# Two interleaved input products, wider zero matmuls, a shifted job queue and one more pre-scaled norm chunk in a two-layer decoder trunk

## The chip, the cores and the metric

The kernel runs on one core of one Trainium2 chip. The metric is the device time of one launch in microseconds (us), as a median over runs. PE is the matrix engine (PEld its weight loads), DVE the vector engine, ACT the scalar engine, POOL the GpSimd engine, and SP the queue from which most transfers are issued.

## The reference, cut to what matters

The input `x` has 256 positions and 2048 channels, all in float32. Two layers follow each other, each ending in a residual and a LayerNorm.

```python
# layer 0: one wide input projection feeds two head groups
z, xbc, dt, q, k, v, gate = split(x @ w_in)
xbc = silu(causal_depthwise_conv(xbc, conv_w, conv_b))   # 4 taps
xs, B, C = split(xbc)                                    # B, C: 4 groups x 128 states
y_a = rms_norm((ssd_scan(xs, dt, B, C) + d * xs) * silu(z))
y_b = moba_attention(rotary(q), rotary(k), v) * silu(gate)
x = layer_norm(alpha * x + concat(y_a, y_b) @ w_out)
# layer 1: diagonal complex state space mixer
u, gate = split(x @ w_in1)
y = gelu(s5(u, lam_re, lam_im, log_dt, b, c) + d * u)
ga, gb = split(y @ w_glu)
x = layer_norm(alpha * x + ((ga * sigmoid(gb)) * silu(gate)) @ w_out1)
```

B and C are the columns called `b` and `c` below, 512 columns each.

## The kernel before, in words

Every large product is float32 made of three single-pass matmuls: both operands are split into a high part (a copy rounded to the matrix engine's fast format) and a low part (the rest), and high·high, high·low and low·high are added up. Weights come in *units* of 128 x 1024 numbers (512 KB): two contraction tiles of 128 rows by 512 output columns. `split_to(i)` (lines 205 to 229) issues the transfer of each unit up to the i-th into a `raw` tile, makes `wh` on ACT (line 225) and `wl` on DVE (line 227). There are four buffers of each. It is called three units ahead of the one that PE works on. For unit 0 the same is done in two halves (lines 216 to 218), each together with one tile of `x` (`xpart`, lines 411 to 413).

`product("w", ...)` runs over the eight units of one block of 512 columns and calls `wmm` (line 288): 24 matmuls per unit, each of 128 x 128 weights against 256 positions, into two PSUM banks. Two pairs of banks alternate from product to product. `product("x", ...)` (line 271) has the operands the other way round: 12 matmuls of 512 columns per unit.

The first product makes `b`, the second `c`, four more make `xs`, four make `z`, then 16 make q, k, v and gate. While the first product runs, `x` arrives in pieces of two tiles (`xpiece`, lines 397 to 403): the dictionary `early` puts piece i ahead of unit i, and piece 5 also issues the constants and parameters.

All other work hangs in a queue of jobs. After each unit `pump` takes as many jobs off the queue as are needed to empty it by the end of the product, and `run` (line 243) places a job behind the split of the unit two ahead. A scheduler then orders each engine's instructions. The jobs that matter here are: four convolution taps and a SiLU per 512 columns (`conv_jobs`, ACT line 506, DVE line 509), the `dt` product and softplus (`dt_mm` lines 424 to 431, `dt_jobs` lines 443 to 493), the C·B masks (`cb_job`, lines 530 to 534), and the tables of the second layer (`trig_job` lines 551 to 575, `table_job` lines 581 on). Later, `block_jobs` build the second layer's matrices block by block; each of 16 blocks loads 256 KB of parameters into one buffer (`bc<-in_s5bc`, line 650).

PE starts with `warm(WARM0)` (line 367): 70 matmuls of zeros, 64 x 64, into an unused bank.

Between the layers lies a border. The last output product of layer 0 (`product_apart`) finishes rows 0 to 127 (t = 0) first and rows 128 to 255 (t = 1) afterwards. `after0` adds the residual (line 973), takes statistics (line 974, 990 to 993) and scales 512-column chunks of the normed row in two DVE steps (`scaled`, lines 1013 and 1016). `turned` transposes a chunk on PE (line 358) and splits it on ACT (line 1026) and DVE (line 1030). For t = 1 PE has to wait for this chain, and `warm(WARM1)` and `warm(WARM2)` put 30 and 4 further matmuls of zeros there. The first product of layer 1 starts when the first chunks are turned; `rest0` turns the remaining half chunk between the terms of its unit 0, and `later` turns further chunks ahead of units 1, 3 and 5, as `step(t, chunk)`, which is `scaled` and then `turned`.

Of the kernel before, what the change touches and what calls it, by code (L numbers as in the profile page):

```python
# [9 lines left out]
F32 = mybir.dt.float32  # L10
F32R = mybir.dt.float32r
AF = mybir.ActivationFunctionType
OP = mybir.AluOpType
# [3 lines left out]
P = 128  # L17
# [3 lines left out]
UK = 2  # L21
CU = KT // UK
ALPHA = 4.0 ** 0.25
NKEEP = 6
WARM0 = 70
WARM1 = 30
WARM2 = 4
EPS = 1e-5
# [65 lines left out]
def _layout(inp):  # L94
# [15 lines left out]
    a["wi0"] = np.concatenate([_chunk(m) for m in cols], 0)  # L110
    w = f["out0_w"][0].reshape(32, P, D)
# [48 lines left out]
def trunk(tc, io, out):  # L160
# [8 lines left out]
    with ExitStack() as top:  # L169
# [30 lines left out]
        nsplit = [0]  # L200
        early = {}
        splits = {}
        keep = [None, range(0)]

        def split_to(i):
            while nsplit[0] <= min(i, len(units) - 1):
                n = nsplit[0]
                if n in early:
                    early.pop(n)()
                raw = st.tile([P, UK, 512], F32, tag="raw", name=nm("raw"))  # L210
                if n == 0:
                    wh = st.tile([P, UK, 512], F32R, tag="wh", name=nm("wh"))
                    wl = st.tile([P, UK, 512], F32R, tag="wl", name=nm("wl"))
                    for k in range(UK):
                        xpart(k)
                        nc.sync.dma_start(raw[:, k, :], units[n][:, k * 512 : k * 512 + 512])
                        A.activation(wh[:, k, :], raw[:, k, :], AF.Copy)
                        V.tensor_tensor(wl[:, k, :], raw[:, k, :], wh[:, k, :].bitcast(F32), op=OP.subtract)
                    ready[n] = (wh, wl)
                    nsplit[0] += 1  # L220
                    continue
                nc.sync.dma_start(raw.rearrange("p k n -> p (k n)"), units[n])
                pool, th, tl = (keep[0], f"wh{n % 8}", f"wl{n % 8}") if n in keep[1] else (st, "wh", "wl")
                wh = pool.tile([P, UK, 512], F32R, tag=th, name=nm("wh"))
                high = A.activation(wh, raw, AF.Copy)  # L225
                wl = pool.tile([P, UK, 512], F32R, tag=tl, name=nm("wl"))
                splits[n] = (high, V.tensor_tensor(wl, raw, wh.bitcast(F32), op=OP.subtract))  # L227
                ready[n] = (wh, wl)
                nsplit[0] += 1
# [42 lines left out]

        def wmm(ps, u, nu, hl, wpair, late=None):
            pv = [p.rearrange("p (f n) -> p f n", n=S) for p in ps]
            wh, wl = wpair
            steps = [(j, o) for j in range(UK) for o in range(4)]
            if u == nu - 1:
                steps = [(j, o) for o in range(4) for j in range(UK)]
            for terms in ((0, 2), (1,)) if late else ((0, 1, 2),):
                if late and terms == (1,):  # L280
                    late()
                for j, o in steps:
# [8 lines left out]

        def product(kind, hl, nu=CU, prelude=None, late=None):
            ps = banks()
            for u in range(nu):
# [4 lines left out]
                if kind == "w":  # L299
                    wmm(ps, u, nu, hl, wpair, late if u == 0 else None)  # L300
                else:
# [59 lines left out]
        idle = cst.tile([P, 64], F32R, name="idle")  # L361
        G.memset(idle.bitcast(F32), 0.0)

        def warm(n):
            px = aux()
            for i in range(n):
                T.matmul(px[:64, 0:64], idle, idle, start=i == 0, stop=i == n - 1)  # L367

# [12 lines left out]
        with ExitStack() as l0:  # L381
# [24 lines left out]
            for i in range(1, CU):  # L406
                early[i] = xpiece(i)

# [108 lines left out]
            cT = a4([P, 4, S])  # L517
            ps = product("w", xhl)
            conv_jobs(ps, 0, bT)
            jobs.append(dt_mm)  # L520
            jobs.extend(dt_jobs())
            ps = product("w", xhl)
            conv_jobs(ps, 4, cT)
            fmem = big("F", [P, 4096])
            cbm = fmem[:, 0:1536].rearrange("p (g n) -> p g n", g=4)

            def cb_job(g):
# [7 lines left out]
                return go  # L535

            for g in range(4):
                jobs.append(cb_job(g))

# [185 lines left out]

            jobs.extend([trig_job, table_job])
            xs = big("C", [P, 2, D])
# [3 lines left out]
            def xs_jobs(ps, j):  # L731
# [263 lines left out]
        with ExitStack() as lt:  # L995
# [41 lines left out]
            def after0(ps, t):  # L1037
# [289 lines left out]
```

## Time and profile before

| what | value |
| --- | --- |
| time, median of 3 runs | 1364.88 us (1363.3 to 1366.78) |
| the profiled execution's own time | 1366.41 us |
| its span, first to last instruction | 1364.6 us |
| PE busy | 1349.1 us in 9918 matmuls |
| DVE, ACT, POOL busy | 982.8, 673.3, 372.3 us |
| transfers | 283.02 MB, mean 207 GB/s |
| mean granted PE clock | 0.995 |

A row of the timeline has the start, the length, the engine, the source line, the operation, output and input, the count, and in brackets how long the engine had been idle and what ended that. The length of a matmul in such rows is modelled and overlaps the next one; what PE really needs per matmul is the distance between two starts. A row of the windows view gives a stretch and its length, then for each engine the busy time and the number of instructions, and at the end the granted PE clock, the share of the transfer engines and GB/s. A row of the chain gives start, length and the instructions that followed each other without a gap.

### The profile page before, as it was taken

To read this page: it belongs to the slowest core of one execution; us is meant where nothing else is said; L and a number is where in the kernel's file an instruction comes from. 1 tells how busy PE (TensorE), PEld (TensorE's weight loads), DVE (VectorE), ACT (ScalarE), POOL (GpSimd) and SP (SyncE) were. 2 spreads that over 40 slices of the span, in tenths; PEclk is the share of its full clock that TensorE was granted. 3 is DMA by queue.
4 is the path that set the end of the run, shared out by engine and by line. 5 is a ranking of instruction groups with operands and counts; after the bars stand their busy time and mean duration, and the time that the engine had idled before them with its cause. 6 is when DMAs were issued, how large, how long until landed. Compare 5 with 4: busy or idle time off the path is not lost.

```text
span 1364.6 us, 25068 instructions
## 1 busy us (share of the span) xinstructions
PE 1349.1 (99%) x9918; PEld 1214.1 (89%) x9918; DVE 982.8 (72%) x1559; ACT 673.3 (49%) x869; POOL 372.3 (27%) x649
## 2 busy tenths in 40 slices
PE   9999999999999999999999999999999999999996
PEld 9999999998998998998988888899977788888885
DVE  5789746687688779689788766748788856555555
ACT  5565557764543543554554344344344545444441
POOL 0140000123027628616788700013243100000001
PEclk9999999999999999999999999899999999999998
DMA  8556555545546756756767779397888666666762
GB/s 308 173 156 201 176 169 166 155 140 170 184 125 208 254 164 205 261 169 207 256 203 229 216 231 315 121 303 247 288 269 300 210 211 191 187 189 187 256 215 78
DMA packets 80742, 283.02 MB, mean 207 GB/s; under 512 B 9840, under 2 KB 12528, under 8 KB 80112
## 3 DMA queue, kind: packets, MB, share of 16 engines
q1 hardware_dynamic: 68112, 239.33, 55.5%
q0 software_dynamic: 7328, 30.42, 6.8%
q10 hardware_dynamic: 5184, 11.67, 2.2%
q8 instruction: 78, 1.28, 0.4%
q14 instruction: 40, 0.33, 0.1%
HBM read 260.41 MB, written 20.97 MB: 206 GB/s over the span
## 4 chain that ended last, share of the span: by engine, by line
PE 94%; DVE 4%; DMA 1%; issue 1%; ACT 0%; POOL 0%; POOLq 0%; DVEq 0%
PE main L288 43%; PE main L271 43%; DVE wl L227 1%; PE aux L358 1%; PE enc L1131 1%; PE aux L794 1%; PE dec L1176 1%; PE aux L701 1%; PE aux L367 1%; DMA bc<-in_s5bc 1%; PE aux L906 1%; PE aux L874 1%; PE aux L764 0%; PE dec L1172 0%; PE aux L697 0%
## 5 line engine op out<-in xcount | busy, mean ns | idle before, releaser
L227 DVE TENSOR_TENSOR wl<-raw,wh 128x1024 fp32r<-128x1024 f32 x431 | 538.5, 1251 | 329.5 <-ACT wh L225 323.4
L225 ACT ACTIVATE wh<-raw 128x1024 fp32r<-128x1024 f32 x431 | 456.1, 1059 | 579.1 <-PE main L271 266.0
L288 PE MATMUL main<-A,wh 128*128 128x256 f32 x1408 | 402.6, 286 | 0.0
L288 PE MATMUL main<-B,wh 128*128 128x256 f32 x1408 | 400.1, 284 | 0.0
L288 PE MATMUL main<-A,wl 128*128 128x256 f32 x1408 | 399.9, 284 | 0.0
L288 PEld LDWEIGHTS main<-A,wh 128*128 128x128 f32 x1408 | 270.8, 192 | 0.6 <-issue 0.2
L288 PEld LDWEIGHTS main<-B,wh 128*128 128x128 f32 x1408 | 270.8, 192 | 0.4
L288 PEld LDWEIGHTS main<-A,wl 128*128 128x128 f32 x1408 | 270.7, 192 | 0.2 <-issue 0.2
L271 PE MATMUL main<-wl,A 128*128 128x512 f32 x512 | 200.4, 391 | 0.5 <-DVE wl L227 0.3
L271 PE MATMUL main<-wh,A 128*128 128x512 f32 x512 | 200.4, 392 | 0.0
L271 PE MATMUL main<-wh,B 128*128 128x512 f32 x512 | 200.0, 391 | 0.0
L271 PE MATMUL main<-wh,C 128*128 128x512 f32 x384 | 152.0, 397 | 0.0
L271 PE MATMUL main<-wh,F 128*128 128x512 f32 x384 | 150.0, 391 | 0.0
L271 PE MATMUL main<-wl,C 128*128 128x512 f32 x384 | 149.8, 390 | 0.0
L635 POOL TENSOR_TENSOR c<-c 128x8 f32<-128x8 f32 (+2 forms) x192 | 108.0, 581 | 28.8 <-DMA wb<-c 21.3
L271 PEld LDWEIGHTS main<-wl,A 128*128 128x128 f32 x512 | 96.2, 188 | 20.9 <-DVE wl L227 1.3
L271 PEld LDWEIGHTS main<-wh,B 128*128 128x128 f32 x512 | 96.2, 188 | 19.9
L271 PEld LDWEIGHTS main<-wh,A 128*128 128x128 f32 x512 | 96.2, 188 | 19.8 <-issue 0.2
L271 PEld LDWEIGHTS main<-wh,C 128*128 128x128 f32 x384 | 72.1, 188 | 15.5
L271 PEld LDWEIGHTS main<-wh,F 128*128 128x128 f32 x384 | 72.1, 188 | 15.4
L271 PEld LDWEIGHTS main<-wl,C 128*128 128x128 f32 x384 | 72.1, 188 | 14.3
L804 POOL TENSOR_TENSOR ssq<-ssq,c 128x256 f32<-128x256 f32 x16 | 17.6, 1099 | 210.2 <-ACT c L802 209.6
(279 smaller groups left out, 1680.6 us busy)
## 6 DMA issues: line engine op xcount, KB each, us to landing
raw<-in_wi SPq DMA_DIRECT2D x271, 512.0 KB, 4.0
raw<-in_wo SPq DMA_DIRECT2D x96, 512.0 KB, 4.3
raw<-in_wglu SPq DMA_DIRECT2D x64, 512.0 KB, 3.7
wt<-wb POOLq DMA_DIRECT2D x16, 896.0 KB, 7.6
wb<-ob ACTq DMA_DIRECT2D x16, 512.0 KB, 5.5
bc<-in_s5bc SPq DMA_DIRECT2D x16, 256.0 KB, 4.4
wb<-c POOLq DMA_DIRECT2D x16, 256.0 KB, 4.1
wb<-om ACTq DMA_DIRECT2D x16, 128.0 KB, 4.1
```

The lines of the kernel that those rows point to most:

```text
L225: high = A.activation(wh, raw, AF.Copy)
L227: splits[n] = (high, V.tensor_tensor(wl, raw, wh.bitcast(F32), op=OP.subtract))
L271: T.matmul(ps[o], l[:, k, sl], r[:, j, :], start=start and i == 0, stop=stop and i == 2)
L288: T.matmul(pv[o // 2][:, o % 2, :], l[:, j, sl], r[:, k, :], start=first and i == 0 and o % 2 == 0, stop=end and i == 2 and o % 2 == 1, sk ...
L358: end = T.transpose(dst[:, i * P : i * P + P], s, ident)
L367: T.matmul(px[:64, 0:64], idle, idle, start=i == 0, stop=i == n - 1)
L635: G.tensor_tensor(p[:, :, :, 0:m], cs[:, :, :, 1 : m + 1], cs[:, i, :, n : n + 1].unsqueeze(1).to_broadcast([P, 2, 4, m]), op=OP.mult)
L701: T.matmul(pk[at : at + 64, a * 16 : a * 16 + 16], ev[:, a, 64 * i : 64 * i + 64], cv[:, a, i, :], start=True, stop=True)
L794: T.matmul(yo, xs[:, 0, xc], df[:, i, 0:256], start=True, stop=False)
L804: G.tensor_tensor(ssq, ssq, jk[:, f, :], op=OP.add)
L874: T.matmul(px[:, 128:384], qT[:, h, P:S], kT[:, h, :], start=True, stop=True)
L906: T.matmul(po, v[:, 0, hs], pT[:, i, 0:256], start=True, stop=False)
```

## The change

The weight blocks `b` and `c` are no longer two products one after the other. A new function runs them together: units b0, c0, b1, c1, b2, c2, b3, c3, then b4 to b7, then c4 to c7, so that a piece of `x` serves two units. The pieces of `x` move in the queue accordingly, ahead of units 2, 4, 6, 8, 9, 10 and 11, and each is placed behind the transfer of the unit before it. In the first four units the matmuls that need `wl` come last, and unit 0 is done tile by tile.

The jobs of `b` are queued when b7 is done and run under c4 to c7; those of `c`, and `dt`, run under the first `xs` product. The masks, `trig_job` and `table_job`, which ran there, are now queued behind the taps of the first, second and third `xs` product, and so run under the second, third and fourth. Jobs are also placed behind the issue of a unit's transfer, not its split alone.

The zero matmuls become 128 x 128 weights against 512 columns, and their numbers change from 70, 30 and 4 to 8, 14 and 3; the zeros are written by DVE and not by POOL.

At the border, the third 512-column chunk of t = 0 is scaled in `after0` already, so that ahead of unit 3 only its transposes and splits are left.

```diff
-WARM0 = 70
-WARM1 = 30
-WARM2 = 4
+WARM0 = 8
+WARM1 = 14
+WARM2 = 3
+PAIRED = 4
...
-    cols = [b, c, xs, z]
+    cols = [xs, z]
...
+    b, c = _chunk(b), _chunk(c)
+    first = np.stack([b[:PAIRED], c[:PAIRED]], 1).reshape(-1, P, UK * 512)
+    a["wi0"] = np.concatenate([first, b[PAIRED:], c[PAIRED:]] + [_chunk(m) for m in cols], 0)
...
                 if n in early:
-                    early.pop(n)()
+                    with tc.issue_after(loaded[-1].ins):
+                        early.pop(n)()
...
-                splits[n] = (high, V.tensor_tensor(wl, raw, wh.bitcast(F32), op=OP.subtract))
+                splits[n] = (loaded[-1], high, V.tensor_tensor(wl, raw, wh.bitcast(F32), op=OP.subtract))
...
+        def product_two(hl, after):
+            pss = [banks(), banks()]
+            order = [(n, u) for u in range(PAIRED) for n in range(2)] + [(n, u) for n in range(2) for u in range(PAIRED, CU)]
+            for at, (n, u) in enumerate(order):
+                split_to(at + 3)
+                parts = (((0, 1), (0, 1)), ((0, 1), (2,)))
+                if at == 0:
+                    parts = tuple(((j,), t) for j in range(UK) for t in ((0, 1), (2,)))
+                wmm(pss[n], u, CU, hl, ready.pop(at), parts if at < 4 else WHOLE)
+                unit[0] += 1
+                pump(CU - 1 - u)
+                if u == CU - 1:
+                    after(pss[n], n)
...
-        G.memset(idle.bitcast(F32), 0.0)
+        V.memset(idle.bitcast(F32), 0.0)
...
-                T.matmul(px[:64, 0:64], idle, idle, start=i == 0, stop=i == n - 1)
+                T.matmul(px, idle[:, 0:1].to_broadcast([P, P]), idle.unsqueeze(1).to_broadcast([P, 8, 64]), start=i == 0, stop=i == n - 1)
...
-                early[i] = xpiece(i)
+                early[2 * i if i < PAIRED else PAIRED + i] = xpiece(i)
...
-            ps = product("w", xhl)
-            conv_jobs(ps, 0, bT)
+
+            product_two(xhl, lambda ps, n: conv_jobs(ps, 4 * n, (bT, cT)[n]))
             jobs.append(dt_mm)
             jobs.extend(dt_jobs())
-            ps = product("w", xhl)
-            conv_jobs(ps, 4, cT)
...
-            for g in range(4):
-                jobs.append(cb_job(g))
...
-            jobs.extend([trig_job, table_job])
...
                 held.extend([back(0), back(1)])
+                jobs.extend({0: [cb_job(g) for g in range(4)], 1: [trig_job], 2: [table_job]}.get(j, []))
...
-                jobs.append((lambda: scaled(1, 2, 2)) if t else (lambda: scaled(0, 4, 4)))
+                jobs.extend([lambda: scaled(1, 2, 2)] if t else [lambda: scaled(0, 4, 4), lambda: scaled(0, 8, 4)])
...
-            later = {1: [(1, 1)], 3: [(0, 2), (1, 2)], 5: [(0, 3), (1, 3)]}
-            first1 = product("w", x1hl, prelude=lambda u: [step(t, i) for t, i in later.get(u, [])], late=rest0)
+            later = {1: [(1, 1)], 3: [(1, 2)], 5: [(0, 3), (1, 3)]}
+            first1 = product("w", x1hl, prelude=lambda u: [turned(0, 8, 4) if u == 3 else None] + [step(t, i) for t, i in later.get(u, [])], first=(((0, 1), (0, 2)), rest0, ((0, 1), (1,))))
```

More of the change, by code (lines that the diff above doesn't have):

```diff
@@ L201, in trunk @@
         early = {}
+        loaded = []
         splits = {}
@@ L215, in split_to @@
                         xpart(k)
-                        nc.sync.dma_start(raw[:, k, :], units[n][:, k * 512 : k * 512 + 512])
+                        loaded.append(nc.sync.dma_start(raw[:, k, :], units[n][:, k * 512 : k * 512 + 512]))
                         A.activation(wh[:, k, :], raw[:, k, :], AF.Copy)
@@ L271, in xmm, with wmm @@
                 T.matmul(ps[o], l[:, k, sl], r[:, j, :], start=start and i == 0, stop=stop and i == 2)
-        def wmm(ps, u, nu, hl, wpair, late=None):
+        WHOLE = (((0, 1), (0, 1, 2)),)
+        def wmm(ps, u, nu, hl, wpair, parts=WHOLE):
             pv = [p.rearrange("p (f n) -> p f n", n=S) for p in ps]
             wh, wl = wpair
[L276 to L281, printed above, removed]
+            for part in parts:
+                if callable(part):
+                    part()
+                    continue
+                js, terms = part
+                steps = [(j, o) for j in js for o in range(4)]
+                if u == nu - 1:
+                    steps = [(j, o) for o in range(4) for j in js]
                 for j, o in steps:
@@ L290, in wmm, with product @@
                                  skip_group_check=True)
-        def product(kind, hl, nu=CU, prelude=None, late=None):
+        def product(kind, hl, nu=CU, prelude=None, first=WHOLE):
             ps = banks()
@@ L299, in product @@
                 if kind == "w":
-                    wmm(ps, u, nu, hl, wpair, late if u == 0 else None)
+                    wmm(ps, u, nu, hl, wpair, first if u == 0 else WHOLE)
                 else:
```

3 lines of the change are left out of this document (1 added, 2 removed).

## The prediction

> **What bounds the kernel now.** I read the page first, then the chain, then the timeline of the two places where PE is not at its pace.
>
> ```profile
> PE 1349.1 (99%) x9918; PEld 1214.1 (89%) x9918; DVE 982.8 (72%) x1559; ACT 673.3 (49%) x869; POOL 372.3 (27%) x649
> PE 94%; DVE 4%; DMA 1%; issue 1%; ACT 0%; POOL 0%; POOLq 0%; DVEq 0%
> ```
>
> PE bounds it. But a busy PE need not be at its pace, so here are stretches of the chain in which nothing disturbs it:
>
> ```profile
> 57.22 28.79 PE main L288 x240
> 887.77 27.82 PE main L288 x232
> 1277.28 76.22 PE main L271 x336
> ```
>
> 28.79 us / 240 is 0.120 us for a matmul of 256 columns, and 76.22 / 336 is 0.227 us for one of 512. Nearly all of the span runs so; only the start and the border between the layers don't. The start:
>
> ```profile
> 0.94 7.68 PE L367 MATMUL aux<-idle 128*64 128x64 f32 x70 [0.94 <-POOL idle L362]
> ...
> 3.82 0.63 ACT L217 ACTIVATE wh<-raw 128x512 fp32r<-128x512 f32 x1 [0.38 <-DMA raw<-in_wi]
> ...
> 4.48 0.69 DVE L218 TENSOR_TENSOR wl<-raw,wh 128x512 fp32r<-128x512 f32 x1 [0.58 <-ACT wh L217]
> ...
> 7.09 0.63 ACT L217 ACTIVATE wh<-raw 128x512 fp32r<-128x512 f32 x1 [2.33 <-DMA raw<-in_wi]
> ...
> 7.75 0.69 DVE L218 TENSOR_TENSOR wl<-raw,wh 128x512 fp32r<-128x512 f32 x1 [2.24 <-ACT wh L217]
> ...
> 8.43 0.56 PE L288 MATMUL main<-A,wh 128*128 128x256 f32 x1
> ...
> 9.06 1.06 ACT L225 ACTIVATE wh<-raw 128x1024 fp32r<-128x1024 f32 x1 [0.69 <-DMA raw<-in_wi]
> ...
> 10.15 1.23 DVE L227 TENSOR_TENSOR wl<-raw,wh 128x1024 fp32r<-128x1024 f32 x1 [1.06 <-ACT wh L225]
> ...
> 10.99 1.06 ACT L225 ACTIVATE wh<-raw 128x1024 fp32r<-128x1024 f32 x1 [0.36 <-DMA raw<-in_wi]
> ...
> 12.21 0.41 PE L288 MATMUL main<-A,wl 128*128 128x256 f32 x1
> ...
> 12.42 0.35 PE L288 MATMUL main<-A,wh 128*128 128x256 f32 x1
> ...
> 12.95 1.06 ACT L225 ACTIVATE wh<-raw 128x1024 fp32r<-128x1024 f32 x1 [0.38 <-DMA raw<-in_wi]
> ```
>
> The reader is to see two losses. The first half tile of weights is split at 4.45 (3.82 + 0.63), yet the zeros hold PE until 8.43. And from 8.43 to 12.42 a matmul starts every 0.213 us (12.21 to 12.42), 18 in 3.99 us: PE runs at half pace, and the 70 narrow zeros had not cured that. The border:
>
> ```profile
> 860.47 0.75 DVE L1016 SCALAR_TENSOR_TENSOR D<-D,mr,row 128x512 f32<-128x512 f32 x1
> ...
> 861.98 1.03 PE L358 MATMUL aux<-consts,D 128*128 128x128 f32 x8
> ...
> 863.25 1.29 DVE L1030 TENSOR_TENSOR F<-aux,C 128x512 fp32r<-128x512 f32 x2 [2.03 <-ACT C L1026]
> ...
> 864.23 1.88 PE L367 MATMUL aux<-idle 128*64 128x64 f32 x30
> ...
> 867.38 0.44 PE L358 MATMUL aux<-consts,D 128*128 128x128 f32 x2 [1.27 <-DVE D L1016]
> ...
> 867.86 0.38 ACT L1026 ACTIVATE C<-aux 128x256 fp32r<-128x256 f32 x1 [1.28 <-PE aux L358]
> ...
> 868.30 0.39 PE L288 MATMUL main<-C,wh 128*128 128x256 f32 x1 [0.27 <-ACT C L1026]
> ...
> 871.08 0.63 PE L358 MATMUL aux<-consts,D 128*128 128x128 f32 x2
> ...
> 871.74 0.38 ACT L1026 ACTIVATE C<-aux 128x256 fp32r<-128x256 f32 x1 [3.50 <-PE aux L358]
> ...
> 872.50 0.74 DVE L1013 SCALAR_TENSOR_TENSOR D<-D,mr,row 128x512 f32<-128x512 f32 x1
> ...
> 878.22 0.68 DVE L1030 TENSOR_TENSOR F<-aux,C 128x512 fp32r<-128x512 f32 x1
> ...
> 878.96 0.38 PE L288 MATMUL main<-F,wh 128*128 128x256 f32 x1 [0.88 <-DVE F L1030]
> ```
>
> ```profile
> 868.00:870.00 2.00, 1.73 (x12) 1.71 (x12) 0.67 (x2) 0.24 (x1) 0.00 (x0) 0.82 0.00 0
> 870.00:872.00 2.00, 2.00 (x11) 2.00 (x11) 0.00 (x0) 0.26 (x1) 0.00 (x0) 0.50 0.00 0
> 872.00:874.00 2.00, 2.00 (x16) 2.00 (x16) 1.80 (x4) 0.89 (x2) 0.00 (x0) 0.82 0.00 0
> ...
> 878.00:880.00 2.00, 1.12 (x8) 1.04 (x8) 2.00 (x4) 0.03 (x1) 0.00 (x0) 0.89 0.73 217
> 880.00:882.00 2.00, 2.00 (x11) 2.00 (x11) 2.00 (x4) 0.00 (x0) 0.00 (x0) 0.50 0.53 205
> 882.00:884.00 2.00, 2.00 (x16) 2.00 (x15) 0.90 (x2) 0.69 (x1) 0.42 (x1) 0.76 0.00 0
> ```
>
> The granted clock falls to 0.50 twice: after the gap that ends at 867.38 and after the one that ends at 878.96. Each time it lasts about 3.4 us, worked out from the shares below 1: (0.18 + 0.50 + 0.18) x 2 us, over the half that is lost, is 3.4 us, and (0.11 + 0.50 + 0.24) x 2 us is the same. Between them PE waits for a chain on DVE (872.50 to 878.90).
>
> **The start, part by part.** Eight zeros of 512 columns at half pace take 8 x 2 x 0.213 = 3.4 us (a 512-column one estimated as two of 256), from 0.94 to 4.36, just before the first split at 4.45. Writing the zeros on DVE and not on POOL costs nothing: both stand idle there. Unit b0 is done tile by tile: 12 matmuls from 4.45, over by 7.0 even at 0.213; 12 more from 7.72 (7.09 + 0.63), eight at once and four behind the low split at 8.44, over by 9.2.
>
> Unit c0 needs no piece of x, so 1280 KB lie up to its end in the queue, against 1536 KB for the second unit before. The splits of units at 9.06, 10.99 and 12.95 mark landings after 1536, 2304 and 3072 KB: 2.5 us per 1000 KB. So c0 lands at about 8.4 (bounds 7.7 and 9.06), is split high by 9.47 and low by 10.75. Its 16 matmuls without `wl` take until 11.4 and the other 8 until 12.35. From there 1280 KB (3.2 us) feed two units (5.76 us), and PE never waits again. So matmul 49 starts at 12.35. Before, 30 matmuls after the nineteenth at 12.42, it starts at 16.0. That is 3.7 us. With c0 landing at 9.06 it is 3.0. If the wide zeros leave PE at half pace until 12.42, only 12 + 22 matmuls are done by then against 18, a gain of 16 x 0.12 = 1.9. I take 3.3, since PE still idles from about 5.9 to 7.7 and half pace may return for a part.
>
> [...]
>
> **What moves behind it.**
>
> ```profile
> 33.35 0.28 PE L288 MATMUL main<-A,wh 128*128 128x256 f32 x1
> ```
>
> ```profile
> 44.35 0.47 DVE L509 SCALAR_TENSOR_TENSOR a<-main,params,a 128x253 f32<-128x253 f32 x1
> ```
>
> ```profile
> 100.00:120.00 20.00, 20.00 (x169) 20.00 (x168) 19.18 (x45) 11.58 (x13) 0.00 (x0) 1.00 0.62 181
> ```
>
> ```profile
> 419.29 0.29 DVE L656 TENSOR_TENSOR bb<-bc,wri 128x128 f32<-128x128 f32 x1 [2.68 <-DMA bc<-in_s5bc]
> ```
>
> ```profile
> bc<-in_s5bc SPq DMA_DIRECT2D x16, 256.0 KB, 4.4
> ```
>
> The taps of b took from the end of product b (33.35) to 44.82, 11.5 us. They had eight units before their banks were written again; now they have four, 4 x 24 x 0.12 = 11.5 us. Their last two taps sit in the second bank, first written 6 matmuls (0.7 us) into the next product. So the cover is 0.7 us; gone, it costs one wait of at most one unit, 2.9 us, once. I take 0.
>
> The 32 matmuls of `dt`, the 16 of the masks and the turns are the same number in another place: 0. Masks, trig and tables spread from one product over three. With DVE busy 19.18 of 20 us PE still passed 169 instructions, so their present crowding costs PE nothing, and thinning it gains nothing; bounds plus and minus 0.5.
>
> On SP the x pieces go behind the unit transfers (counted above), the constants follow four units later than before and still well ahead of their first use in the taps, `wdt` and `s5p` move with their jobs, and 7 of the 16 loads of `bc` (with both of the first residual) stand one or two unit transfers further back, the first of them 117. Behind a unit transfer they are still issued four units (11 us) ahead of their DVE work, against a landing of 4.4 us. One load came 2.68 us late before, and PE did not wait. I take 0.
>
> **The border.** 14 zeros x 0.227 = 3.18 us run from 864.23 to 867.41, against 867.38 where the transposes stood ready: 0. Three more take 0.68 from about 867.6 and end at 868.28, against 868.30: 0, at most 0.2. PE is then dense until the first main matmul, and the first fall of the clock should go. 16 matmuls take 1.92 and not the 2.78 up to 871.08, and ACT follows the transposes by 0.48 (867.38 to 867.86) and not 0.66 (871.08 to 871.74): the DVE chain starts 1.0 earlier. Its next instructions up to the low split at 878.22 are as many as before, since of the third chunks only t = 0 left and t = 1 moved up. So main matmuls go on at 877.95, not 878.96.
>
> The two steps of the chunk scaled ahead (2 x 0.75 us) go into DVE's idle 2.03 us before 863.25: 0. Behind 877.95 the transposes for unit 4 are done already, and PE has 94 matmuls and 8 transposes up to the end of the sixth unit: 94 x 0.12 + 0.9 = 12.2, thus 890.1. Before, it was 887.77 + 46 x 0.12 = 893.3. But PE still idles some 2 us before 877.95; if the clock falls again, 3.4 us hold 16 matmuls in place of 28, a loss of 1.5. Gain 1.7 with the fall, 3.2 without; without the first mending too, 0.7. I take 1.6.
>
> **Sum.** 3.3 + 1.6 = 4.9 us. The profiled execution took 1366.41 (span 1364.6 and 1.8 around it) and would take 1361.5. It lies 1.5 above the median of 1364.88, which would come to 1360.0.
>
> **The rivals.** *The clock does not fall in the short gaps:* 3.7 + 3.2 = 6.9, so 1358.0. Against it speak the two falls above, after gaps under 2 us. [...]
>
> *Zeros do not count as activity, however wide:* then 1.9 + 0.7 = 2.6, so 1362.3. For it: neither 70 nor 30 narrow ones helped. Against it: narrow ones fill PE only in part (64 columns every 0.11 us, where 256 take 0.213 at the same pace).
>
> *Slower:* the `bc` loads that stand further back come too late, DVE waits for them with the unit splits queued behind, and PE waits for the splits. To reach 0.3% above before, about the least that a measurement of this kernel can tell from no change (4.1 us), 7 loads must cost PE (4.1 + 4.9) / 7 = 1.3 us each, which gives 1369.0. Against it: the late one above cost PE nothing.
>
> *It does nothing:* x pieces and weights still arrive together and the zeros only change width; 1364.9.
>
> **How the numbers follow.** Forecast 0.50, clock stays up 0.20, zeros don't count 0.19, nothing 0.04, slower 0.07. Faster than 1360.8 are the second case and some three quarters of the first: 0.57. Slower 0.07. The rest, 0.36, lies within 0.3%. The range leaves out "nothing" and "slower" and takes in the ends at 1358.0 and 1362.3 with a spread of about 1 us between runs: 1357.2 to 1363.4.
>
> **What would show it.** Right: main matmuls from about 4.5, 0.12 apart before 9; matmul 49 near 12.4; no clock of 0.50 between 868 and 872 on the scale of before; transposes for unit 4 ahead of the DVE wait. Wrong: starts 0.213 apart after the wide zeros; a PE wait for `wh` of the second or third unit beyond 10; zeros that end after DVE's chunk at the border; a PE wait for taps at the first `xs` product, or for `wl` behind a `bc` load.

## The result, and the profile after

The changed kernel takes 1360.99 us (median of 7 runs, 1358.89 to 1361.99). The kernel before took 1364.88 us beside it. The ratio is 0.9968, with a 95% interval of 0.9958 to 0.9978, so it is faster by 3.0 to 5.7 us. The forecast was 1360.0, with a range of 1357.2 to 1363.4. The profiled execution took 1361.99 us (span 1360.2), 4.4 less than the 1366.41 of the one before.

From the page of the kernel after, the busy times of PE and the chain's shares:

```profile
PE 1344.3 (99%) x9839; PEld 1206.9 (89%) x9839; DVE 982.5 (72%) x1560; ACT 674.0 (50%) x870; POOL 363.2 (27%) x648
PE 94%; DVE 4%; DMA 1%; issue 1%; ACT 0%; SPq 0%; POOL 0%; POOLq 0%; DVEq 0%
```

PE bounds it as before. The 79 matmuls that are gone are zeros (70 + 30 + 4 less 8 + 14 + 3). To see where time went I use three rows of the chain that stand for the same work in every kernel: 192 matmuls near 343 us, 180 near 493, and the last long row. First the kernel before, then the kernel after:

```profile
346.20 23.03 PE main L288 x192
496.00 21.60 PE main L288 x180
```

```profile
342.52 23.03 PE main L297 x192
492.81 21.60 PE main L297 x180
1272.88 76.22 PE main L276 x336
```

The last row of the kernel before stands in the prediction (1277.28). So the start of the first row gives what the start of the kernel is worth: 346.20 - 342.52 = 3.68 us gained. From there to the second row it was 149.80 us and is 150.29: 0.49 lost. From the second to the third, which holds the border, it was 781.28 and is 780.07: 1.21 gained. Together 4.40.

The start, in the timeline of the kernel after:

```profile
0.99 3.78 PE L390 MATMUL aux<-idle 128*128 128x512 f32 x8 [0.99 <-DVE idle L385]
...
4.56 0.43 PE L297 MATMUL main<-A,wh 128*128 128x256 f32 x1
4.83 0.27 PE L297 MATMUL main<-B,wh 128*128 128x256 f32 x1
4.95 0.28 PE L297 MATMUL main<-A,wh 128*128 128x256 f32 x1
...
6.84 0.51 PE L297 MATMUL main<-A,wh 128*128 128x256 f32 x2 [0.55 <-ACT wh L222]
...
8.34 1.06 ACT L230 ACTIVATE wh<-raw 128x1024 fp32r<-128x1024 f32 x1 [1.55 <-DMA raw<-in_wi]
...
9.45 0.39 PE L297 MATMUL main<-A,wh 128*128 128x256 f32 x1 [0.91 <-ACT wh L230]
...
12.43 0.28 PE L297 MATMUL main<-A,wh 128*128 128x256 f32 x1
```

PE begins at 4.56 instead of 8.43, at 0.12 us per matmul from the second on (4.83 to 4.95). It then waits twice, 0.55 us for the second half of unit b0 and 0.91 us for c0, which lands at 8.34. Matmul 49 starts at 12.43.

The border, in the timeline and in the windows of the kernel after (the third last column is the granted clock):

```profile
861.03 3.38 PE L390 MATMUL aux<-idle 128*128 128x512 f32 x14
...
864.38 0.93 PE L390 MATMUL aux<-idle 128*128 128x512 f32 x3
865.15 0.33 PE L297 MATMUL main<-C,wh 128*128 128x256 f32 x1
...
874.74 0.38 PE L297 MATMUL main<-F,wh 128*128 128x256 f32 x1 [1.35 <-DVE F L1048]
```

```profile
862.00:872.00 10.00, 10.00 (x74) 9.16 (x72) 7.34 (x15) 2.74 (x5) 0.00 (x0) 1.00 0.01 2
...
872.00:874.00 2.00, 1.24 (x8) 0.72 (x6) 2.00 (x4) 1.80 (x4) 0.00 (x0) 1.00 0.52 160
874.00:876.00 2.00, 1.26 (x7) 1.26 (x8) 2.00 (x5) 0.00 (x0) 0.00 (x0) 0.79 0.74 197
876.00:878.00 2.00, 2.00 (x12) 2.00 (x11) 1.86 (x3) 0.00 (x0) 0.00 (x0) 0.50 0.41 168
878.00:880.00 2.00, 2.00 (x16) 2.00 (x16) 0.00 (x0) 0.90 (x1) 1.50 (x6) 0.86 0.19 29
```

The first fall of the clock is gone: PE is dense from 861 to 872, at a granted clock of 1.00. The second is there, behind a gap of 1.35 us in which PE waits for DVE. And between the two, the loads of `bc`, in the timeline and in the chain of the kernel after, then in the chain of the kernel before:

```profile
416.38 0.29 DVE L674 TENSOR_TENSOR bb<-bc,wri 128x128 f32<-128x128 f32 x1 [3.45 <-DMA bc<-in_s5bc]
...
432.03 0.50 PE L276 MATMUL main<-wl,A 128*128 128x512 f32 x1 [0.23 <-DVE wl L232]
```

```profile
408.26 8.10 DMA bc<-in_s5bc
```

```profile
411.94 7.33 DMA bc<-in_s5bc
```

DVE waits 3.45 us for the load (2.68 before), and its other work queues up behind it: the splits of weights (`wl`) and parts of the second layer's matrices (`kt`, `et`). PE's weight loads wait for these. Their waits between 405 and 445 us in the kernel after, in total, times and longest:

```profile
PEld main L276 <- DVE wl L232: 1.0, 2, 0.7
PEld aux L734 <- DVE kt L726: 0.5, 1, 0.5
PEld aux L715 <- DVE et L695: 0.4, 1, 0.4
```

In both kernels the chain runs through this load.

### The profile page after: what moved, and what is told of

It is laid out like the page before. It is cut to its first block, busy times and chain, and to the rows that moved or that the text cites. A ratio compares the mean times of both kernels' runs of the same rounds, so it can differ in the third digit from the quotient of the medians.

```text
span 1360.2 us, 24904 instructions
## 1 busy us (share of the span) xinstructions
PE 1344.3 (99%) x9839; PEld 1206.9 (89%) x9839; DVE 982.5 (72%) x1560; ACT 674.0 (50%) x870; POOL 363.2 (27%) x648
## 3 DMA queue, kind: packets, MB, share of 16 engines
q8 instruction: 77, 1.26, 0.4%
## 4 chain that ended last, share of the span: by engine, by line
PE 94%; DVE 4%; DMA 1%; issue 1%; ACT 0%; SPq 0%; POOL 0%; POOLq 0%; DVEq 0%
PE main L276 43%; PE main L297 43%; DVE wl L232 1%; PE aux L381 1%; PE enc L1149 1%; PE aux L812 1%; PE dec L1194 1%; PE aux L719 1%; DMA bc<-in_s5bc 1%; PE aux L924 1%; PE aux L892 1%; PE aux L782 0%; PE dec L1190 0%; PE aux L715 0%; DMA raw<-in_wi 0%
## 5 line engine op out<-in xcount | busy, mean ns | idle before, releaser
L297 PE MATMUL main<-A,wl 128*128 128x256 f32 x1408 | 395.0, 284 | 0.0
L653 POOL TENSOR_TENSOR c<-c 128x8 f32<-128x8 f32 (+2 forms) x192 | 104.5, 563 | 25.6 <-DMA wb<-c 18.0
L873 POOL TENSOR_TENSOR a<-a,b 64x512 f32<-64x512 f32 x16 | 28.3, 1771 | 169.3 <-DVE b L872 132.2
```

What stands on the lines that cost most here:

```text
L297: T.matmul(pv[o // 2][:, o % 2, :], l[:, j, sl], r[:, k, :], start=first and i == 0 and o % 2 == 0, stop=end and i == 2 and o % 2 == 1, sk ...
L653: G.tensor_tensor(p[:, :, :, 0:m], cs[:, :, :, 1 : m + 1], cs[:, i, :, n : n + 1].unsqueeze(1).to_broadcast([P, 2, 4, m]), op=OP.mult)
L873: turns.append(G.tensor_tensor(q[0:64], q[0:64], tm, op=OP.add))
```

## The experiments

All twelve are set against the same three rows. "Start" is the time of the first row, "middle" the distance from the first to the second, "border" from the second to the third. The wait is DVE's for the second `bc`.

| kernel | time, us | ratio to before (95%) | start | middle | wait | border |
| --- | --- | --- | --- | --- | --- | --- |
| before | 1364.88 | | 346.20 | 149.80 | 2.68 | 781.28 |
| before, second profile | 1365.04 | | 345.71 | 149.91 | 2.73 | 780.29 |
| after | 1360.99 | 0.9968 (0.9958 to 0.9978) | 342.52 | 150.29 | 3.45 | 780.07 |
| after, second profile | 1359.95 | | 342.63 | 149.26 | 1.49 | 778.93 |
| narrow zeros | 1360.36 | 0.9966 (0.9953 to 0.9979) | 342.99 | 149.82 | 2.68 | 778.31 |
| wide zeros alone | 1364.44 | 0.9996 (0.9987 to 1.0006) | 347.37 | 149.01 | 0.53 | 778.76 |
| chunk not ahead | 1360.18 | 0.9963 (0.9950 to 0.9976) | 342.72 | 148.99 | 0.82 | 778.84 |
| third unit | 1358.43 | 0.9949 (0.9932 to 0.9966) | 342.72 | 150.15 | 3.30 | 776.74 |
| third unit, two `bc` | 1357.56 | 0.9943 (0.9929 to 0.9957) | 342.65 | 149.01 | none | 776.75 |
| two `bc` | 1359.04 | 0.9955 (0.9938 to 0.9971) | 342.14 | 149.02 | none | 778.34 |
| no zeros | 1361.51 | 0.9978 (0.9968 to 0.9987) | 342.13 | 149.00 | 0.87 | 780.39 |
| zeros of before | 1361.47 | 0.9975 (0.9965 to 0.9985) | 345.38 | 149.89 | 2.80 | 777.63 |
| jobs back | 1378.26 | 1.0102 (1.0085 to 1.0119) | 361.00 | 149.87 | 2.94 | 778.41 |
| ordinary order | 1362.06 | 0.9986 (0.9976 to 0.9995) | 343.50 | 150.73 | 3.88 | 778.36 |

The three columns come from one profile each. The time is a median of 4 to 10 runs, for the two second profiles a single run; one run of "two `bc`" took 2300.44 us, which the ratio leaves out (the median of the other three is 1358.88). The kernel before was run again beside the experiments: it took 1365.45 us beside "narrow zeros", "wide zeros alone", "chunk not ahead" and "third unit", 1365.11 beside both kernels with two `bc`, "no zeros" and "zeros of before", and 1363.66 beside "jobs back" and "ordinary order". Between these sets the ratios say more than the times.

**Is it the width of the zeros?** In the kernel after, with zeros of 64 columns:

```diff
-WARM0 = 8
-WARM1 = 14
-WARM2 = 3
+WARM0 = 32
+WARM1 = 30
+WARM2 = 4
...
-                T.matmul(px, idle[:, 0:1].to_broadcast([P, P]), idle.unsqueeze(1).to_broadcast([P, 8, 64]), start=i == 0, stop=i == n - 1)
+                T.matmul(px[:64, 0:64], idle, idle, start=i == 0, stop=i == n - 1)
```

> The changed kernel with zero matmuls as narrow as before (64 x 64), 32 at the start (about the same 3.4 us as the 8 wide ones), 30 and 4 at the border. If density opens the clock: main matmuls start near 4.5 but 0.213 us apart until somewhere between 8.5 and 12.4; matmul 49 starts 0.2 to 1.9 us later than in the changed kernel (12.43); at the border the clock falls to 0.50 right behind the first gap again and 0.5 to 1.0 us of the lead is lost. Time 1361.7 to 1363.9. If only the time spent on zeros counts, not their width: 0.12 us apart from 4.5 as in the changed kernel, and 1361.0.

The time is that of the kernel after, and at the border the granted clock does not fall (1.00 from 860 to 884 us, 778.31), both against the first expectation. Its start, in the timeline:

```profile
4.59 0.58 PE L297 MATMUL main<-A,wh 128*128 128x256 f32 x1
4.97 0.41 PE L297 MATMUL main<-B,wh 128*128 128x256 f32 x1
5.18 0.41 PE L297 MATMUL main<-A,wh 128*128 128x256 f32 x1
...
10.15 0.28 PE L297 MATMUL main<-B,wh 128*128 128x256 f32 x1
...
12.90 0.28 PE L297 MATMUL main<-A,wh 128*128 128x256 f32 x1
```

The narrow zeros leave PE at half pace (0.21 us from 4.97 to 5.18), as they did before. But c0 is not split until 9.78 in this run. At half pace the 24 matmuls of b0 fill the time that PE otherwise spends waiting (4.59 and 24 x 0.213 is 9.7), and matmul 49 comes only 0.47 us later, 12.90 against 12.43. Most of that is the landing of c0, 0.38 us later in this profile (its split starts at 8.72, not 8.34). So width is not what the start's gain rests on.

The same width in the kernel before, and nothing else of the change:

```diff
-WARM0 = 70
-WARM1 = 30
-WARM2 = 4
+WARM0 = 8
+WARM1 = 14
+WARM2 = 3
...
-                T.matmul(px[:64, 0:64], idle, idle, start=i == 0, stop=i == n - 1)
+                T.matmul(px, idle[:, 0:1].to_broadcast([P, P]), idle.unsqueeze(1).to_broadcast([P, 8, 64]), start=i == 0, stop=i == n - 1)
```

> The kernel before with nothing changed but the zero matmuls (8, 14 and 3 of 512 columns). If the two causes at the start are apart: PE starts near 4.5 at full clock and then waits for x and weights of each unit, with matmul 49 near 14.3, a lead of 1.8 us instead of 3.64; at the border the first fall of the clock is gone and main matmuls go on 1.0 us earlier, a lead of 1.0 to 1.2. Sum 2.8 to 3.0: 1361.9 to 1362.1. If the zeros alone do it and the order of the transfers does nothing: 3.6 at the start and 1361.0 or less. If the interleaving is all: 1364.9.

No change in time: 0.9996. Its start is 1.2 us later than before (347.37 against 346.20), in spite of a first matmul at 4.56. The timeline tells why:

```profile
11.17 0.58 PE L288 MATMUL main<-A,wh 128*128 128x256 f32 x1 [2.57 <-ACT wh L225]
11.55 0.41 PE L288 MATMUL main<-B,wh 128*128 128x256 f32 x1
11.77 0.41 PE L288 MATMUL main<-A,wh 128*128 128x256 f32 x1
```

PE starts early at full pace (0.12 us from 4.78 to 4.90), uses up its unit, and waits 2.57 us for the next one, which shares the queue with a piece of `x`. Behind the wait it runs at half pace again, 0.21 us per matmul, and the granted clock is 0.50 from 12 to 14 us. The early start is lost to the gap and to the half pace behind it. The border is 1.5 to 2.5 us shorter than in the two profiles of before, and the middle had a punctual `bc` in this profile; over the runs nothing is left of it.

Then both other corners of that square, in the kernel after. First no zeros at all:

```diff
-            warm(WARM0)
...
-            warm(WARM1)
...
-            with tc.issue_after(end.ins):
-                warm(WARM2)
```

> The kernel after with no zero matmuls at all, neither at the start nor at the border. Theory: the start is paced by the landing of the pieces of x and of the raw weights, and the clock of its first products matters little: PE begins with the first piece, full clock comes some 3.4 to 5.5 us later, the 49th matmul runs at 12.4 to 13.0 us (after 12.43, with narrow zeros 12.90) and the first use of `bc` lies at 387.2 to 388.0. At the border PE is idle for some 4 us, so that the clock is half for about 3.4 us behind it: 1.7 us lost against a run whose clock stays, 0.3 against the profile of after. Together 1361.0 to 1363.0. Rival: the wide zeros carry the start's gain; then the first use of `bc` is at 389 or later and the time 1363.5 or more.

```profile
4.49 0.58 PE L297 MATMUL main<-A,wh 128*128 128x256 f32 x1 [4.49 <-ACT wh L222]
4.87 0.41 PE L297 MATMUL main<-B,wh 128*128 128x256 f32 x1
...
8.46 0.28 PE L297 MATMUL main<-A,wh 128*128 128x256 f32 x1
8.57 0.28 PE L297 MATMUL main<-B,wh 128*128 128x256 f32 x1
...
12.04 0.28 PE L297 MATMUL main<-A,wh 128*128 128x256 f32 x1
```

Without zeros the start is as good as with them (342.13, against 342.14 to 342.72 in the six profiles with the change's own start), and matmul 49 runs at 12.04. At the border PE stands idle 3.0 us for DVE and the granted clock is 0.50 from 862 to 868 us: 780.39 instead of 778.3, so about 2 us are what the zeros are worth there. As expected, and the rival (the zeros carry the start) falls.

And then the zeros of before, 70, 30 and 4 of 64 columns:

```diff
-WARM0 = 8
-WARM1 = 14
-WARM2 = 3
+WARM0 = 70
+WARM1 = 30
+WARM2 = 4
...
-                T.matmul(px, idle[:, 0:1].to_broadcast([P, P]), idle.unsqueeze(1).to_broadcast([P, 8, 64]), start=i == 0, stop=i == n - 1)
+                T.matmul(px[:64, 0:64], idle, idle, start=i == 0, stop=i == n - 1)
```

> The kernel after with the zeros of before in number and shape (70, 30 and 4 of 64 columns). Theory: the 70 zeros hold PE until about 8.5 us and leave the clock at half, so that 24 to 36 matmuls wait behind them and run 0.213 us apart until the clock rises 3.4 to 5.5 us later; the 49th matmul runs at 14.5 to 16.0 us against 12.43 and 16.07, the first use of `bc` is at 389.0 to 391.0, and the time is 1362.0 to 1364.5. Rival: the order of the loads and of the first products is all that counts; then the 49th matmul runs before 13.0 us and the time is that of after, 1361.0.

The start is at 345.38: with the units in turns, 70 zeros cost 2.9 us against the kernel after, because they hold PE until 8.48. So neither part does it alone: against the first profile of before, turns with the old zeros gain 0.8 us (346.20 to 345.38), short zeros without turns lose 1.2, and both together gain 3.7. (The second profile of before starts 0.5 earlier, which shifts all three alike.) The time, 1361.47, is nearer to the kernel after than the start alone would make it. That is the border: in this build the scheduler put the second pair of transposes ahead of the first main matmuls instead of behind sixteen of them, and the border took 777.63 although the granted clock fell once (0.50 from 868 to 870 us). I did not expect that, and I have not tried it alone.

Last, the order inside the first four units:

```diff
-                wmm(pss[n], u, CU, hl, ready.pop(at), parts if at < 4 else WHOLE)
+                wmm(pss[n], u, CU, hl, ready.pop(at), WHOLE)
```

> The kernel after with its two products still in turns, but every unit's matmuls in their ordinary order, so that each product of three needs the low part of the weights at once. The first matmul then runs until the low half at about 5.2, and the units stall where `wl` is made, 1.2 to 1.3 us behind `wh`. Theory: of the start's 3.7 us about 0.7 to 1.3 is lost; the 49th matmul starts near 13.5 and the first use of `bc` is at 388.0 to 388.5, the time 1361.5 to 1362.5. Rival: order inside a unit does not count, as the landings pace it; the time is that of after, 1361.0, and the first use of `bc` at 386.9 to 387.4.

The start is at 343.50, 0.8 to 1.4 us later than with the change's order (342.14 to 342.72), since PE now waits for `wl` (0.52 us at 10.65, others too short to be listed). The 0.8 is against "third unit", in which the third and fourth units are split at the same times to 0.01 us (11.43 and 12.71). The middle lost more, 150.73, behind a late `bc`. By the ratios the kernel is 2.5 us above the kernel after (0.9986 against 0.9968); only the start's part of that can be put down to this edit, and whether the edit makes the load later is not shown.

**The moved jobs.** The masks, `trig_job` and `table_job` queued under the first `xs` product again:

```diff
-                jobs.extend({0: [cb_job(g) for g in range(4)], 1: [trig_job], 2: [table_job]}.get(j, []))
+            jobs.extend([cb_job(g) for g in range(4)] + [trig_job, table_job])
             for j in range(4):
                 ps = product("w", xhl)
```

> The kernel after with the masks, the trigonometry and the tables of the second layer queued under the first `xs` product again, behind the taps of c and `dt`. Theory, the prediction's step of 0 with its bounds of 0.5: the crowding moves DVE and ACT and not PE; the lead on the kernel before that the start gives is still there at the first use of `bc`, which lies at 387.4 less or plus 0.5, and the time is 1360.5 to 1361.5. Rival: DVE falls behind under the first `xs` product, the splits of the weights come late, PE waits for `wl` between 45 and 100 us, and the first use of `bc` is at 388 or later, the time above 1362.

This is the largest effect of all, and neither number expected it: 1378.26 us, 17 above the kernel after (18.5 at the first row, 361.00 against 342.52). Windows (per stretch: PE, PEld, DVE, ACT, POOL, the granted clock, then transfers) and timeline of this kernel:

```profile
100.00:110.00 10.00, 6.91 (x40) 6.16 (x38) 4.46 (x7) 2.81 (x4) 5.32 (x6) 0.83 0.37 113
110.00:120.00 10.00, 1.74 (x9) 1.18 (x7) 8.31 (x34) 6.78 (x15) 0.00 (x0) 0.64 0.18 53
120.00:130.00 10.00, 7.32 (x47) 7.35 (x48) 8.51 (x30) 4.22 (x5) 0.00 (x0) 0.68 0.01 2
```

```profile
106.25 0.31 PE L513 MATMUL aux<-consts,ew 32*128 32x32 f32 x1 [3.09 <-DVE ew L499]
...
122.68 0.55 PE L297 MATMUL main<-A,wh 128*128 128x256 f32 x1 [8.93 <-DVE a L532]
```

PE is idle for 14.0 of these 30 us (10 - 6.91, 10 - 1.74 and 10 - 7.32), and the granted clock is 0.83, 0.64 and 0.68 in them. It waits first for the softplus of `dt` (3.09 us, behind a long run of instructions on POOL), and at the end 8.93 us for the taps of the first `xs` product, which stand behind the trigonometry in DVE's queue. In the kernel after PE is busy 10.00 of 10.00 us in all three stretches. The rival was right that DVE falls behind; that it is the taps and not `wl` which PE waits for was in neither.

**The border.** The third chunk scaled late, as before:

```diff
-                jobs.extend([lambda: scaled(1, 2, 2)] if t else [lambda: scaled(0, 4, 4), lambda: scaled(0, 8, 4)])
+                jobs.append((lambda: scaled(1, 2, 2)) if t else (lambda: scaled(0, 4, 4)))
...
-            later = {1: [(1, 1)], 3: [(1, 2)], 5: [(0, 3), (1, 3)]}
+            later = {1: [(1, 1)], 3: [(0, 2), (1, 2)], 5: [(0, 3), (1, 3)]}
...
```

> The changed kernel without the chunk scaled ahead. If the lead at the border comes from the clock: main matmuls of the third unit go on at the same place, the transposes of the third chunk come behind them again, and 0.4 to 0.7 us are lost: 1361.4 to 1361.7. If it comes from the relief of DVE: the whole lead of the border, 1.4 us, is lost: 1362.4.

The border takes 778.84, as in "wide zeros alone" (778.76), and 778.31 to 778.41 with the chunk ahead and no fall of the clock (four profiles). So the chunk is worth 0.4 to 0.5 us. In the time it does not show (0.9963 against 0.9968).

Is the second fall a property of the kernel after? The same kernel once more:

> The kernel after, unchanged, for a second profile of it. Theory: whether the clock falls behind the gap of 1.35 us at the border is not a property of the program. The same gap has now been followed by a fall in one profile of the kernel after, and by none in four variants that leave this gap alone. So the likelier picture is no fall, a granted clock of 1.00 from 876 to 880 us, a border of 55.4 us (first scale to first result of the next product) instead of 57.11, and 1359 to 1361 us. Rival: the program sets it; then the granted clock shows 0.50 there again and the border takes 57.1.

Timeline and windows of this second profile:

```profile
873.82 0.39 PE L297 MATMUL main<-F,wh 128*128 128x256 f32 x1 [1.33 <-DVE F L1048]
```

```profile
872.00:874.00 2.00, 0.67 (x4) 0.46 (x4) 2.00 (x4) 0.90 (x2) 0.00 (x0) 1.00 0.71 246
874.00:876.00 2.00, 2.00 (x18) 2.00 (x19) 2.00 (x4) 0.00 (x0) 0.00 (x0) 1.00 0.86 244
```

The same gap, and the granted clock stays at 1.00. The border takes 778.93; 0.6 us of that is a wait for a transfer near 910, so 778.3 without it.

And the kernel before once more:

> The kernel before, unchanged, for a second profile of it. Theory: the first fall of the clock is likely, as narrow zeros stood behind a fall in two of three profiles and wide ones in none of six; the second is not certain. With two falls the border takes 58.3 us, with one 56.6. The wait for `bc` is also not a property of the program: 2.68 us or under 1 us, as 0.53 was seen with the same loads. Rival: all of it repeats, 58.3 and 2.68.

```profile
868.00:870.00 2.00, 2.00 (x10) 2.00 (x11) 0.32 (x1) 0.00 (x0) 0.00 (x0) 0.55 0.00 0
870.00:872.00 2.00, 2.00 (x13) 2.00 (x12) 0.00 (x0) 0.13 (x1) 0.00 (x0) 0.60 0.00 0
```

One fall in place of two, and a border of 780.29 instead of 781.28. The wait for `bc` did repeat, 2.73 us, against my expectation for that part. With narrow zeros the first fall was there in three of four profiles (not in "narrow zeros"), with wide ones in none of nine.

What would take the gap itself away: the third unit's low half `F` is what PE waits for, so its 16 matmuls that don't read it go first:

```diff
-        def product(kind, hl, nu=CU, prelude=None, first=WHOLE):
+        def product(kind, hl, nu=CU, prelude=None, first=WHOLE, third=WHOLE):
...
-                    wmm(ps, u, nu, hl, wpair, first if u == 0 else WHOLE)
+                    wmm(ps, u, nu, hl, wpair, {0: first, 2: third}.get(u, WHOLE))
...
-            first1 = product("w", x1hl, prelude=lambda u: [turned(0, 8, 4) if u == 3 else None] + [step(t, i) for t, i in later.get(u, [])], first=(((0, 1), (0, 2)), rest0, ((0, 1), (1,))))
+            first1 = product("w", x1hl, prelude=lambda u: [turned(0, 8, 4) if u == 3 else None] + [step(t, i) for t, i in later.get(u, [])], first=(((0, 1), (0, 2)), rest0, ((0, 1), (1,))), third=(((0, 1), (0, 2)), ((0, 1), (1,))))
```

> The changed kernel, and in the third unit of the first product of the second layer the 16 matmuls that don't need the low half of x come first. If the wait of 1.35 us for that half and the second fall of the clock hang together: both go, 2.5 to 2.9 us off, 1358.1 to 1358.5. If the clock falls for another reason (the transposes ahead of it): 1.35 off and the fall stays, 1359.6. If the wait only moves on to the next chunk: 1361.0 to 1360.6.

```profile
872.00:874.00 2.00, 1.86 (x15) 1.49 (x14) 2.00 (x3) 1.90 (x4) 0.00 (x0) 1.00 0.59 145
874.00:876.00 2.00, 2.00 (x19) 2.00 (x18) 2.00 (x5) 0.00 (x0) 0.00 (x0) 1.00 0.71 174
```

PE is idle for 0.14 us where it stood idle for 1.5 (2 - 1.24 and 2 - 1.26), the granted clock stays at 1.00, and the border takes 776.74. The time is 1358.43, some 2.5 us under the kernel after.

**The `bc` loads.** Two buffers instead of one, first in the kernel after, then on top of the third unit's change:

```diff
-                    bc = h["bc"] = pp.tile([P, 4, 8, 16], F32, tag="bc", name=nm("bc"))
+                    bc = h["bc"] = pp.tile([P, 4, 8, 16], F32, tag="bc", bufs=2, name=nm("bc"))
```

> The kernel after, with two buffers for `bc` and nothing else. Theory: the wait of 3.45 us goes and the stretch between the first and the fourth use of `bc` falls from 77.75 to about 76.45 us: 1361.0 less 0.8 to 1.3 is 1359.7 to 1360.2, with the border's clock adding or taking up to 1.4 us in one profile. Rival: PE loses nothing to the wait, and the time is that of after, 1361.0.

> The kernel after, with the third unit's 16 matmuls not waiting for the low half first, and with two buffers for `bc`. Theory: a late `bc` load does cost PE. In the six profiles so far the stretch from the first block's use of `bc` to the fourth's took 76.45 and 76.46 us where the load was waited for 0.8 us or less, and 77.25 to 77.75 us where it was waited for 2.7 to 3.5 us. With a second buffer the wait is 0.8 us or less, the stretch 76.4 to 76.6 us, and the time 0.8 to 1.3 us under that of the third unit's change alone (1358.43): 1357.1 to 1357.6. Rival, the prediction's own step: the wait costs PE nothing; the wait goes, and the time stays at 1358.4 (1358.0 to 1358.8).

The wait is gone and the middle takes 149.02 and 149.01. Of the waits of the weight loads shown above none is left in "two `bc`". Counted from start to start, the matmuls of the kernel after lose some 1.6 us between 408 and 440 us against their undisturbed pace, and those of "two `bc`" 0.4 over the same work. The chain of "two `bc`" runs through PE where it ran through the load:

```profile
404.73 8.47 PE main L297 x69
413.20 10.91 PE main L276 x48
```

The other profiles say the same without the edit. The middle takes 148.99 to 149.01 wherever DVE waits 0.9 us or less, and it grows with the wait: 149.26 at 1.49 us, 149.80 to 149.91 at 2.7 to 2.9, 150.15 and 150.29 at 3.3 and 3.5, 150.73 at 3.88. The rival (the wait costs PE nothing) falls. The times, 1359.04 and 1357.56, are 2.0 and 0.9 us under those without the edit; 1.1 to 1.3 is what the middle explains. The rest of the 2.0 may be the clock, which did not fall at the border in that profile (1.00 from 860 to 890 us, 778.34); over the runs that is not shown. The intervals of the ratios overlap (0.9938 to 0.9971 and 0.9958 to 0.9978), so it is the middle that shows the gain, more than the times. The last kernel, 1357.56 us, is the best: 0.9943 of the kernel before.

## Why the prediction was right, and where it was not

The sum was 3.3 + 0 + 1.6 = 4.9 us. The two pairs of profiles measured 3.68 - 0.49 + 1.21 = 4.40, and, for the second profiles, 3.08 + 0.65 + 1.36 = 5.09. By the medians the gain is 3.9 (1364.88 less 1360.99). So the total was right; three of the reasons behind it were not, the role of the clock at the start, the reason for the moved jobs and the late `bc` load. That the total comes so near owes something to luck: a fall of the clock at the border is worth 1.0 to 1.5 us and the late load up to 1.7, and both differ between profiles of one and the same kernel.

*The start, 3.3.* The working holds point by point. The first matmul was forecast at 4.45 and came at 4.56; c0 landing at 8.4, 8.34; c0 split high by 9.47, 9.40 (8.34 + 1.06); matmul 49 at 12.35, 12.43. What fell is the role of the clock. Behind the wide zeros PE was to be at full pace, and in this profile it is, 0.12 us per matmul from 4.83 on; behind the narrow ones of "narrow zeros" it is not (0.21 from 4.97). Even that is partly luck. With the same eight zeros matmuls start 0.21 us apart up to 7.15 in "third unit":

```profile
5.00 0.42 PE L297 MATMUL main<-B,wh 128*128 128x256 f32 x1
5.22 0.42 PE L297 MATMUL main<-A,wh 128*128 128x256 f32 x1
```

They do so up to 6.0 in "two `bc`" and 7.0 in "jobs back" too. This is the prediction's own sign of being wrong, starts 0.213 apart after the wide zeros, and yet the first rows of "third unit" and "two `bc`", 342.72 and 342.14, lie about where that of the kernel after lies (342.52). So full pace from the first units on is worth 0.47 us of matmul 49 at most, and nothing in the run without zeros. The lower bound of 1.9 was built on it and was no bound: it let half pace last until 12.42, while in the run without zeros the matmuls of the product itself were at full pace after 4.0 us (4.49 to 8.46). And it forgot that PE at full pace only waits: 0.55 and 0.91 us for transfers. So the rival "zeros do not count" priced the start wrongly too. What the start rests on is the hold that is taken off PE (2.9 us, zeros of before) and the turns that keep it fed (without them a loss of 1.2), and on neither alone.

How long PE must work before it is at full pace is not one number in these runs. In the run without zeros it took 4.0 us of matmuls of 256 columns. The eight wide zeros, some 3.6 us, were enough in some profiles and not in others. Behind 7.68 us of narrow zeros the kernel before still ran at 0.213 us per matmul, up to 12.42.

*The moved jobs, 0.* The number is right for the change as a whole: PE never waits between 20 and 130 us. The reason given is wrong: "their present crowding costs PE nothing, and thinning it gains nothing". That was read from the schedule of before, in which `dt` ran under product c. With the turns `dt` comes to lie under the first `xs` product as well, and had masks and tables stayed there, it would have cost 17 to 18 us. The bounds of plus and minus 0.5 were for a state that the change itself removes.

*The `bc` loads, 0.* This step failed: "the late one above cost PE nothing". I had looked for a PE wait near the late load and found none worth the name. The chain of before has that very load in it, 411.94 for 7.33 us, and that means the end of the run hung on it. It cost 0.8 us before (149.80 against 149.0) and 1.3 after (150.29). The loss lies in the short waits of the weight loads for `wl`, `kt` and `et`; of these the list of PE's own waits names one, the 0.23 us at 432.03. How late the load comes differs from one profile to the next of the same kernel (3.45 and 1.49 after), so that the change cannot be said to make it worse. As a rival for "slower" it stayed far below its price of 1.3 us for each of seven loads, since only one load is late.

*The border, 1.6.* Measured 1.21 and 1.36. The parts were right: the first fall gone; the DVE chain 1.0 us earlier, so that main matmuls go on 12.05 us after the scale of t = 1 and not 13.07 (874.74 - 862.69 after, 878.96 - 865.89 before, where the second number is the row of its statistics), which on the old scale is 877.94 (874.74 and the lead of 3.20 at that point), against 877.95 in the forecast; a gap that is still there and may still lower the clock. The forecast held the second fall for the likely case. It is one of the two: it came in one profile of the kernel after and not in the other, and in none of the six other kernels with a gap of 1.33 to 1.35 us there, nor in the second profile of before, whose second gap is 1.35 us. Without any fall the border takes 778.35, 2.9 us less than the first profile of before, where the prediction had 3.2.

The gap alone does not tell whether the clock falls. Behind the gap of 1.35 us it fell in the kernel after, and 1.33 us in its second profile left it at 1.00. The falls behind gaps of 1.27 us say less of the gap: 1.88 us of narrow zeros stand ahead of the gap in the kernel before, and from 864.23 to 868.30, 4.1 us, PE had little but them to do. Nor does the fall come at one distance behind the gap: 0.42 us in the kernel after (from 874.74 to 875.16), 1.92 and 0.58 us in the kernel before (from 867.38 to 869.30 and from 878.96 to 879.54). What decides whether the same gap is followed by a fall, no run here shows.

## What to carry to other kernels

A late transfer that stands in the chain can cost the end of the run (0.8 and 1.3 us in the first profiles here), even where no wait of the bound engine names it: read the chain and the waits of the weight loads for it, not only the waits of the matmuls. When a change moves one job under another product, price the jobs that were already there again; "it cost nothing before" holds only for the neighbours that it had before. And before a warm-up of the clock is tuned, see whether the stretch behind it is paced by the clock or by the landing of data: here the zeros at the start were worth nothing once data arrived in the right order (first row at 342.13 without them, 342.14 to 342.72 with).

## What the runs showed of the hardware that was not expected

- Whether the clock falls behind a short gap is not set by the gap alone. The same 1.33 to 1.35 us gap at the border was followed by a granted clock of 0.50 in one profile of the kernel after and by 1.00 in the next. A fall cost 1.0 us (the two profiles of before) to 1.5 (780.07 less 0.2 us of another wait, against 778.35).
- Without zeros the matmuls of 256 columns were at full pace after 4.0 us (4.49 to 8.46); behind 3.6 us of narrow zeros it took 5.6 us more (4.59 to 10.15). One profile of each does not show that narrow zeros delay full pace; it shows that these did not bring it.
- One load of 256 KB comes between 0.5 ("wide zeros alone") and 3.9 us ("ordinary order") late for the same place in the program, and PE loses up to 1.7 us by it (150.73 against 149.0).
